# Rotary embedding on one core: the first tile's load in two pieces, both tables behind the first, in place of three pieces with the tables between them

## The chip, the cores and the metric

The kernel runs on one core of one Trainium2 chip. The metric is the device time of one execution in microseconds (us); the time of a kernel is the median of its runs. Before the change it is 169.99 us, the median of 3 runs that went from 169.5 to 170.23.

The engines that matter here are PE (TensorE, matmul), DVE (VectorE), ACT (ScalarE), POOL (GpSimd) and SP (SyncE), which issues every transfer of this kernel. L72 means line 72 of the kernel.

## The reference

```python
def reference(x, cos, sin, num_heads):      # x (16, 512, 1024), cos and sin (512, 32), 16 heads
    x = x.reshape(batch, seq, num_heads, head_dim)          # head_dim 64
    x1, x2 = (x[..., :half_dim].copy(), x[..., half_dim:].copy())
    cos = cos[None, :, None, :].copy()
    sin = sin[None, :, None, :].copy()
    rotated = np.concatenate([x1 * cos - x2 * sin, x1 * sin + x2 * cos], axis=-1)
    return rotated.astype(np.float32)
```

Each output element is its own input times a cosine, plus the element of the other half of its head times a signed sine. Everything is float32: 33.55 MB go in and as much comes out.

## The kernel before

**Tiles and rows.** The input is cut into 8 tiles of 4 MiB, each 128 partitions by 8192 elements. A partition of a tile holds 8 consecutive sequence positions, called rows here (k = 0 to 7), of 1024 elements (4 KB) each. Every instruction of the main loop works on one row over all partitions. Five tile buffers (BUFS) are kept on the chip, so tiles 0 to 4 are loaded ahead of the loop and tiles 5, 6 and 7 when tile 2 has been stored. The result is written over the input in the same buffer and stored from there, a whole tile at once.

**The order of issues on SP.** All loads and stores go through one queue, issued by SP in the order in which the program has them. The first tile is loaded in pieces given by FIRST, (2, 4, 8): rows 0 and 1, then rows 2 and 3, then rows 4 to 7. The two tables, 64 KiB each, stand in between: the order at the start is rows 0-1, sin (L81), rows 2-3, cos (L83), rows 4-7, tile 1, 2, 3, 4. Schedules are written out by hand (manual_schedule): an engine runs its instructions in program order, and waits are put in where data, a buffer or the semaphore of an earlier transfer require it. An instruction waits for the transfer that brings its row, not for the whole tile.

**The tables.** They arrive on 64 partitions and are needed on 128. A matmul with the 64x128 matrix `spread` copies sin (L105) and then cos (L106) into one PSUM tile, `tab`. DVE then makes the signed sine table `sns` in on-chip memory (L108 the negated half, L109 the other half) and copies the two rows of it that DVE itself needs back into `tab` (L113). POOL's first multiply needs `sns`, DVE's first multiply needs `tab`.

**The main loop.** For each row, DVE multiplies by the cosine into PSUM (L158 or L173). The sine product is made by POOL (L155, into a buffer b of the pool `bp`, which has 6 buffers) or, for row 0 and, in odd tiles, row 3 as well, by DVE (L160, in place). The two are added in one of two ways. For the rows in PE_ROWS (0, 3 and 6) PE adds the sine product into PSUM by a matmul with the identity (L163) and ACT copies the sum to the tile (L166). For the other five rows DVE adds (L145), one instruction or more later (the list `pending`). A tile's store (L76) waits for the last of its eight rows.

**At the start PE runs four matmuls on zeros** (L96), which set the PSUM buffers' accumulation flags.

Of the kernel before, what the change touches and what calls it, by code (L numbers as in the profile page):

```python
# [18 lines left out]

DVE_B = ((0,), (0, 3))  # L20

FIRST = (2, 4, 8)
LAST_OUT = (8,)


# [1 line left out]
def kernel(  # L27
# [40 lines left out]
    def load(t, lo=0, hi=KK):  # L68
        if tiles[t] is None:
            tiles[t] = xp.tile([P, F], FP32, name="xt")  # L70
        s = slice(lo * dim, hi * dim)
        nc.sync.dma_start(out=tiles[t][:, s], in_=x_v[t][:, s])  # L72
# [4 lines left out]

    load(0, 0, FIRST[0])
    sin_sb = bp.tile([P, dim], FP32, name="b")[:PB, : KK * half]
    cos_sb = bp.tile([P, dim], FP32, name="b")[:PB, : KK * half]  # L80
    nc.sync.dma_start(out=sin_sb, in_=sin_v)  # L81
    load(0, FIRST[0], FIRST[1])
    nc.sync.dma_start(out=cos_sb, in_=cos_v)  # L83
    for lo, hi in zip(FIRST[1:], FIRST[2:]):
        load(0, lo, hi)
    for t in range(1, BUFS):
        load(t)
# [59 lines left out]
    for t in range(NT):  # L147
# [31 lines left out]
        else:  # L179
            lo = 0  # L180
            for hi in LAST_OUT:
                store(t, lo, hi)
                lo = hi
# [38 lines left out]
```

## Time and profile before

| what | us |
|---|---|
| median of 3 runs | 169.99 |
| the profiled execution's own time | 169.99 |
| its span (first to last instruction) | 167.8 |
| outside the span | 2.2 |
| DVE busy | 139.6 (83% of the span) |
| POOL busy | 121.4 (72%) |
| PE busy | 84.4 (50%) |
| ACT busy | 25.6 (15%) |
| cos table landed | 9.6 |
| first DVE instruction on a table | 10.9 |
| last DVE instruction ends | 154.5 |
| last store issued | 155.6 |

The span is counted from its first instruction. The landing of a transfer is the time at which SP began to issue it, plus the time from issue to landing that the profile lists for it. DVE is the busiest engine and hardly rests between 10.9 and 154.5 us; the transfers are busy for almost as long, and then the last store of 4 MiB stands alone at the end.

### The profile page before, as it was taken

What the parts mean: (1) busy time and instruction counts of PE and PEld (TensorE: products, weight loads), DVE (VectorE), ACT (ScalarE), POOL (GpSimd) and SP (SyncE); (2) the same over time, 40 slices, a digit from 0 to 9 for tenths busy, and PEclk for the clock granted to TensorE, in tenths of its full rate; (3) what the DMA queues carried; (4) which work ended last, traced back from release to release, by engine and by line L of the source; (5) the groups of instructions that cost most, each with busy time, mean ns of one, the idle gap of its engine ahead of it and who ended that gap; (6) DMA issues with size and microseconds to landing.
All of it is one profiled execution on the core that took longest, in us unless ns stands there. A gap on an engine that the chain in (4) does not pass through costs nothing.

```text
span 167.8 us, 612 instructions
## 1 busy us (share of the span) xinstructions
PE 84.4 (50%) x104; PEld 26.4 (16%) x104; DVE 139.6 (83%) x123; ACT 25.6 (15%) x25; POOL 121.4 (72%) x58
## 2 busy tenths in 40 slices
PE   4224618448418834845746184474488408438000
PEld 1111202202102210210221022012022102202000
DVE  1039999999999899999999999999999999997000
ACT  0003220221121122022112202220211220221000
POOL 1019999999999999989796999867996998000000
PEclk9999995585855595555678955765555985585855
DMA  5999999999999999999999999999999999930885
GB/s 187 392 432 473 406 430 437 406 469 398 477 398 438 414 447 422 437 438 406 469 406 461 414 461 406 455 406 437 430 445 422 414 461 398 477 164 0 375 375 250
DMA packets 2754, 67.26 MB, mean 401 GB/s; under 512 B 320, under 2 KB 448, under 8 KB 448
## 3 DMA queue, kind: packets, MB, share of 16 engines
q1 hardware_dynamic: 2752, 67.24, 93.8%
q14 instruction: 2, 0.02, 0.0%
HBM read 33.69 MB, written 33.55 MB: 401 GB/s over the span
## 4 chain that ended last, share of the span: by engine, by line
DVE 70%; issue 13%; DMA 4%; PE 3%; SPq 1%; ACT 1%; DVEq 0%; ACTq 0%
DVE pd L173 28%; DVE xt L145 23%; DVE ps L158 10%; DVE xt L160 9%; DMA b<-in_cos_dram 4%; PE ps L163 2%; PE tab L106 1%; ACT xt L166 1%; SPq L72 1%; SPq L81 0%; DVEq L145 0%; DVE tab L113 0%; DVE sns L108 0%; DVE sns L109 0%; DVEq L160 0%
## 5 line engine op out<-in xcount | busy, mean ns | idle before, releaser
L155 POOL TENSOR_TENSOR b<-xt,sns 128x1024 f32<-128x1024 f32 x52 | 120.7, 2356 | 19.9 <-DVE sns L109 10.5
L163 PE MATMUL ps<-xt,ident 128*128 128x512 f32 x48 | 42.8, 1045 | 34.1 <-issue 20.1
L163 PE MATMUL ps<-b,ident 128*128 128x512 f32 x48 | 37.3, 922 | 29.3 <-DVE ps L158 18.7
L145 DVE TENSOR_TENSOR xt<-pd,b 128x1024 f32<-128x1024 f32 x40 | 48.9, 1221 | 2.9 <-DVE pd L173 0.5
L173 DVE TENSOR_TENSOR pd<-xt,tab 128x1024 f32<-128x1024 f32 x40 | 49.1, 1228 | 1.1
L166 ACT COPY xt<-ps 128x1024 f32<-128x1024 f32 x24 | 24.3, 1012 | 115.2 <-PE ps L163 105.2
L158 DVE TENSOR_TENSOR ps<-xt,tab 128x1024 f32<-128x1024 f32 x24 | 29.3, 1222 | 0.0
L163 PEld LDWEIGHTS ps<-xt,ident 128*128 128x128 f32 x48 | 13.4, 307 | 62.1 <-issue 57.4
L163 PEld LDWEIGHTS ps<-b,ident 128*128 128x128 f32 x48 | 11.6, 266 | 55.6 <-POOL b L155 30.9
L160 DVE TENSOR_TENSOR xt<-xt,tab 128x1024 f32<-128x1024 f32 x12 | 14.6, 1220 | 0.4
L108 DVE TENSOR_SCALAR sns<-tab 128x256 f32<-128x256 f32 x1 | 0.4, 423 | 9.3 <-PE tab L106 9.3
L166 ACT ACT_TABLE_LOAD x1 | 1.3, 1283 | 14.8 <-DVE xt L160 14.8
L105 PE MATMUL tab<-b,spread 64*128 64x256 f32 x2 | 1.2, 696 | 3.0 <-DMA b<-in_sin_dram 3.0
L96 PE MATMUL ps<-zero 128*128 128x512 bf16 x4 | 1.9, 627 | 1.2 <-DVE zero L92 1.2
L106 PE MATMUL tab<-b,spread 64*128 64x256 f32 x2 | 1.2, 710 | 2.4 <-DMA b<-in_cos_dram 2.4
L105 PEld LDWEIGHTS tab<-b,spread 64*128 64x128 f32 x2 | 0.5, 307 | 3.9 <-issue 3.9
L106 PEld LDWEIGHTS tab<-b,spread 64*128 64x128 f32 x2 | 0.5, 306 | 3.2 <-DMA b<-in_cos_dram 3.2
L92 DVE MEMSET zero<- 128x256 uint32 x1 | 0.3, 272 | 0.9 <-PEq L203 0.9
L96 PEld LDWEIGHTS <-zero 128*128 128x128 bf16 x4 | 0.4, 130 | 1.7 <-DVE zero L92 1.2
L113 DVE COPY tab<-sns 128x64 f32<-128x64 f32 x2 | 0.5, 228 | 0.1
L104 DVE COPY spread<-ident 64x64 f32<-64x64 f32 x2 | 0.3, 182 | 0.2 <-POOL ident masks.py:199 0.2
masks.py:197 POOL MEMSET ident<- 128x128 f32 x1 | 0.2, 205 | 0.3 <-POOLq L203 0.3
(6 smaller groups left out, 1.1 us busy)
## 6 DMA issues: line engine op xcount, KB each, us to landing
out_dram<-xt SPq DMA_DIRECT2D x8, 4096.0 KB, 22.6
xt<-in_x_dram SPq DMA_DIRECT2D x7, 4096.0 KB, 29.5
xt<-in_x_dram SPq DMA_DIRECT2D x2, 1024.0 KB, 6.2
xt<-in_x_dram SPq DMA_DIRECT2D x1, 2048.0 KB, 11.4
b<-in_sin_dram SPq DMA_DIRECT2D x1, 64.0 KB, 4.7
b<-in_cos_dram SPq DMA_DIRECT2D x1, 64.0 KB, 7.3
```

The lines of the kernel that those rows point to most:

```text
L72: nc.sync.dma_start(out=tiles[t][:, s], in_=x_v[t][:, s])
L96: nc.tensor.matmul(out=ps[:, c : c + BANK], lhsT=zero[:, :P], rhs=zero, start=True, stop=True)
L105: nc.tensor.matmul(out=sin_t, lhsT=spread, rhs=sin_sb, start=True, stop=True)
L106: nc.tensor.matmul(out=cos_t, lhsT=spread, rhs=cos_sb, start=True, stop=True)
L113: nc.vector.tensor_copy(out=sns_t[:, i * hd : (i + 1) * hd], in_=sns[:, k])
L145: nc.vector.tensor_tensor(out=r, in0=ps, in1=b, op=ALU.add)
L155: nc.gpsimd.tensor_tensor(out=halves(b), in0=swapped(r, nh), in1=over_heads(sk), op=ALU.mult)
L158: nc.vector.tensor_tensor(out=pairs(ps), in0=pairs(r), in1=cos_b(k), op=ALU.mult)
L160: nc.vector.tensor_tensor(out=halves(r), in0=halves(r), in1=swapped_signed(k), op=ALU.mult)
L163: nc.tensor.matmul(out=ps[:, c : c + BANK], lhsT=ident, rhs=rhs, start=False, stop=True, skip_group_check=True)
L166: nc.scalar.copy(out=r, in_=ps)
L173: nc.vector.tensor_tensor(out=pairs(ps), in0=pairs(r), in1=cos_b(k), op=ALU.mult)
```

## The change

FIRST becomes (3, 8): the first tile comes in two pieces, rows 0 to 2 (1.5 MiB) and rows 3 to 7 (2.5 MiB). Both tables are issued behind the first piece, sin and then cos. SP's order at the start is therefore rows 0-2, sin, cos, rows 3-7, tile 1, 2, 3, 4: one transfer fewer, the same bytes in all. The matmul rows, the buffers, the single last store (LAST_OUT, (8,)) and the order of the instructions on PE, DVE, ACT and POOL are the same in both kernels. In the changed kernel, all lines behind L82 have a number lower by one.

```diff
-FIRST = (2, 4, 8)
+FIRST = (3, 8)
 LAST_OUT = (8,)
...
     nc.sync.dma_start(out=sin_sb, in_=sin_v)
-    load(0, FIRST[0], FIRST[1])
     nc.sync.dma_start(out=cos_sb, in_=cos_v)
-    for lo, hi in zip(FIRST[1:], FIRST[2:]):
+    for lo, hi in zip(FIRST, FIRST[1:]):
         load(0, lo, hi)
```

## The prediction

> **What bounds the kernel now.** I read the page first: busy time of each engine over the span, and the transfers' rate.
>
> ```profile
> DVE  1039999999999899999999999999999999997000
> DMA  5999999999999999999999999999999999930885
> GB/s 187 392 432 473 406 430 437 406 469 398 477 398 438 414 447 422 437 438 406 469 406 461 414 461 406 455 406 437 430 445 422 414 461 398 477 164 0 375 375 250
> ```
>
> A slice is 4.2 us. DVE is idle for two slices, then full for 34, then idle while the last store drains. The transfers are full too, but in slices 35 and 36 they run dry and wait for DVE, so they carry a backlog and do not set the end. By windows of 1 us they moved 164 GB/s from 148 to 149 us and nothing from 149 to 154: the backlog ends near 148.4 us, and the last store is issued at 155.6. An earlier end of DVE becomes an earlier end of the kernel, up to some 7 us.
>
> Next, the chain of work that ended last, at its start:
>
> ```profile
> 2.36 7.27 DMA b<-in_cos_dram
> 9.68 1.23 PE tab L106 x2
> 12.24 1.24 DVE ps L158
> 13.51 1.22 DVE xt L160
> ```
>
> The chain starts with the cos table's transfer (landing at 2.36 + 7.27 = 9.63), goes through its matmul, and then lies on DVE until 150.9, where a matmul, a copy and the last store end it. What starts DVE is thus cos. The timeline of the first 32 us shows why sin, which was there earlier, did not help:
>
> ```profile
> 0.73 0.38 SPq L72 DMA_DIRECT2D xt<-in_x_dram  x1
> ...
> 1.17 0.53 SPq L81 DMA_DIRECT2D b<-in_sin_dram  x1
> ...
> 1.74 0.57 SPq L72 DMA_DIRECT2D xt<-in_x_dram  x1
> ...
> 2.36 0.47 SPq L83 DMA_DIRECT2D b<-in_cos_dram  x1
> 2.87 3.10 SPq L72 DMA_DIRECT2D xt<-in_x_dram  x5
> ...
> 6.05 1.19 PE L105 MATMUL tab<-b,spread 64*128 64x256 f32 x2 [2.97 <-DMA b<-in_sin_dram]
> ...
> 9.68 1.22 PE L106 MATMUL tab<-b,spread 64*128 64x256 f32 x2 [2.44 <-DMA b<-in_cos_dram]
> 10.93 0.42 DVE L108 TENSOR_SCALAR sns<-tab 128x256 f32<-128x256 f32 x1 [9.30 <-PE tab L106]
> ...
> 11.77 20.84 POOL L155 TENSOR_TENSOR b<-xt,sns 128x1024 f32<-128x1024 f32 x9 [10.46 <-DVE sns L109]
> ```
>
> L108 reads only the sine, whose matmul ended at 7.24, but it starts at 10.93, after L106: both halves are one tile, and DVE waits for the second matmul. POOL waits behind it. So the end of L106 gates both engines, and it is the quantity to predict.
>
> **Step 1: where the tables land.** The DMA view, one window for each issue, gives the time to landing:
>
> ```profile
> b<-in_sin_dram SPq DMA_DIRECT2D x1, 64.0 KB, 4.7
> b<-in_cos_dram SPq DMA_DIRECT2D x1, 64.0 KB, 7.3
> xt<-in_x_dram SPq DMA_DIRECT2D x1, 2048.0 KB, 11.4
> ```
>
> Sin landed at 5.9 with 1.05 MB ahead of it (1.11 MB with itself), cos at 9.63 behind 2.23 MB in all. Now sin stands behind 1.57 MB, which is 0.52 MB more. Two rates price these. Windows give 394 GB/s for 4 to 8 us: 0.52/0.394 = 1.3 us, sin at 7.2. Between the two landings, 1.11 MB took 3.7 us (300 GB/s): 1.75 us, sin at 7.65. I take 7.4. Cos follows 0.066 MB later, at 0.2 us by either rate: 7.6. Its issue moves up by one place (1.74 in place of 2.36), in time by far.
>
> By the Trainium skill, "DMA: Bandwidth & Descriptors", section "Anatomy of one DMA", a transfer on another issue path costs about 2.0 us and then goes at 436 GB/s; for all 2.23 MB from the first issue that is 0.73 + 2.0 + 5.1 = 7.8 us for cos, where the trace has 9.63. By that estimate cos would now land at 6.6.
>
> **Step 2: the two table matmuls now run back to back.** Before, L105 hid in the wait for cos. Now both are on the path. L105 starts 0.15 us behind its landing (6.05 against 5.9): 7.55. Its two passes have a mean of 696 ns each and end 1.19 after the start, so passes start about 0.5 us apart. Four passes in a row end 3 x 0.5 + 0.7 = 2.2 us after the first start, at 9.75; if L106 must wait for the end of L105, at 7.55 + 1.19 + 1.22 = 9.96. Against cos's own bound, 7.6 + 1.27 = 8.9, the pair decides. I take 9.8, against 10.90 before (9.68 + 1.22). **The gain at the gate is 1.1 us, from 0.7 (sin at 7.65, no overlap) to 1.4 (sin at 7.2, overlap).** It is half or two thirds of the 1.8 to 2.0 us by which cos comes earlier; the rest goes to L105.
>
> A longer pause of PE speaks against this. PE's zeros end at 3.1, so PE rests 2.97 us before L105; now it rests about 4.5. Does that slow the table matmuls? In the same timeline four passes of 512 columns take 1.96 us in one place and 3.75 in another (L163 at 19.74 and 25.85), 0.49 and 0.94 a pass with the last one's drain shared out; half as many columns would be 0.25 and 0.47. The tables' passes start 0.5 us apart, which is already the slow rate, so there is nothing to lose, although the granted-clock column reads 1.00 there. The Trainium skill, "TensorE: Matmul & The Clock Gate", section "Part 1: The HAM clock gate", says that an idle window of about 3.4 us halves the clock; had the pair run at the fast rate before, its estimate would have been another 1.0 us of PE time, and the gain would be nearly nil.
>
> **Step 3: what hides the rest.** Rows 3 to 7 now come as one transfer. Row 3 came with rows 2-3 (1.74 + 7.5 = 9.2); now it lands with row 7, when the same 4.33 MB are through: 2.87 + 11.4 = 14.3. POOL is the first to need it: its third multiply, at 11.77 + 2 x 2.32 = 16.4 before, 15.3 after. DVE needs it at 18.37 - 1.1 = 17.3. The cover is 1.0 us. Behind it POOL has little: row 7's product is ready at 11.77 + 7 x 2.32 = 28.0 and DVE's add of it starts at 28.20, so 0.2 us later everything moves. Cost nothing, while the piece lands before 15.5; this also caps the gain at 16.6 - 14.3 = 2.3 us. Rows 0-2 land before sin in the same queue.
>
> Tiles 1 to 4 keep their bytes ahead of them; tile 1 lands at 3.52 + 20.5 = 24.0 and POOL needs it at 27.9 - 1.1. SP's wait at the fifth of the last group (0.3 us, for an earlier transfer's semaphore) goes, since there is one transfer fewer; that tile is needed near 71, so nothing follows. Tile 5 is closer: issued at 66.36, it lands 25.6 later at 92.0, and POOL starts it at 92.11. The backlog sets that landing, so POOL will not start tile 5 earlier. But its first product is ready at 94.5, and DVE's add of it starts at 104.3: nine microseconds of cover, cost nothing. DVE's and POOL's instructions are the same, 123 and 58, in the same order.
>
> **Step 4: the end.** The last store waits for ACT's copy of row 6 (154.55 to 155.56), behind four matmul passes of 3.57 us at the slow rate (granted 0.50 to 0.55), and for DVE's last add (153.25 + 1.23 = 154.5). Moved by 1.1 us, these matmuls may meet another clock: at the fast rate (1.96 us) ACT would be 1.6 earlier and DVE's add would decide, 1.1 us earlier; at the slow rate of other places (3.75) 0.2 later. I take no change.
>
> **Sum.** 169.99 - 1.1 = 168.9 us. The profiled execution's own time is 169.99, span 167.8 and 2.2 outside it; that is also the median of the three runs, so nothing is corrected.
>
> **Rivals.**
>
> *Small gain.* One of the 16 DMA engines falls behind in the larger first piece, and sin is as late as 7.9 to 8.3. For it: cos landed 0.9 us later than 394 GB/s would make it from sin's landing (5.9 + 1.11/0.394 = 8.7). Each tenth of sin's lateness beyond 7.4 is a tenth of the gain lost, because L105 and L106 hang on it: 168.9 + 0.5 to 168.9 + 0.9, 169.4 to 169.8.
>
> *Larger gain.* As above, and the last matmuls get the fast clock: 168.9 - 1.1 = 167.8. For it: the row of granted clocks flips between 1.0 and 0.5 all along. Against: it is as likely to flip in the runs of before, which lie within 0.7 us.
>
> *Slower: the 2.5 MiB piece lands late.* If it lands at L, POOL's third multiply starts at L, and beyond 15.5 each microsecond is one on DVE's row 7. The time is 168.9 + (L - 15.5): even at 16.6, slower by 0.85 at 17.5. Against: the windows hold 429 and 446 GB/s from 8 to 16 us; landing at 17.5 would need 4.33 MB at 274 GB/s from the first byte near 1.7, against 344 for the landing at 14.3.
>
> *No effect.* The earlier start is absorbed at tile 5 or by the backlog: 170.0. Against: nine microseconds of POOL's lead, and 7 us in which the transfers run dry.
>
> **How the numbers follow.** Forecast 0.55 (168.5 to 169.3); larger gain 0.12; small gain 0.20; no effect 0.05; slower 0.08. A change of 0.5%, 0.85 us, is what a measurement here can tell from none, so faster means below 169.14. Nearly all of the forecast (0.52) and the larger gain make 0.64 faster; 0.03 of the forecast, the small gain and no effect make 0.28 same; 0.08 slower. The range reaches from the larger gain, 167.7, to no effect, 170.0; left out are the slower case and the tails below.
>
> **What would show it.** Sin's landing near 7.4, with L105 and L106 side by side and ending near 9.8; L108 directly behind them, and DVE's first multiply near 11.1 in place of 12.24; no wait for a transfer on POOL's third multiply; DVE's last add ending near 153.4 and the last store issued near 154.5. The prediction is wrong if sin lands after 8.5, if POOL's third multiply shows a wait for the second piece, or if the last store does not move with DVE's start.

## The result, and the profile after

The changed kernel takes 167.96 us (median of 6 runs, 167.07 to 168.68) against 169.82 for the kernel before, run beside it (6 runs, 169.1 to 170.23). The ratio is 0.989, with a 95% interval of 0.985 to 0.993: faster by 1.8 us, 1.2 to 2.5. The prediction was 168.9, faster, with 167.7 to 170.0 as its range. The direction held and the time lies in the range, but the gain is larger than the 1.1 us that were forecast: the time is below the forecast's own band (168.5 to 169.3) and close to the rival with the larger gain (167.8), which had a chance of 0.12.

The profiled execution after took 167.84 us, with a span of 165.7, against 169.99 and 167.8 before: 2.15 us less. Here is where they come from, first in the busy times and the rate of the transfers by slices of 4.1 us:

```profile
DVE  1069999999999999999999999999999999998000
...
DMA  5999989999899998989999899999999999980885
GB/s 187 388 465 401 491 380 498 388 435 451 380 498 388 427 453 388 498 388 475 404 411 475 388 491 396 437 435 403 475 403 467 411 427 443 403 380 0 380 380 253
```

DVE is full again from the third slice on, and it starts a part of a slice earlier (6 in place of 3). The transfers still run dry before the last store (slice 36 moves nothing), so nothing of the earlier start is lost to them. The timeline of the start shows the gate (start, duration, engine and line, and in brackets the idle time before and what ended it):

```profile
1.17 0.53 SPq L81 DMA_DIRECT2D b<-in_sin_dram  x1
...
1.74 0.58 SPq L82 DMA_DIRECT2D b<-in_cos_dram  x1
2.37 2.62 SPq L72 DMA_DIRECT2D xt<-in_x_dram  x5
7.68 1.19 PE L104 MATMUL tab<-b,spread 64*128 64x256 f32 x2 [4.61 <-DMA b<-in_sin_dram]
8.67 1.06 PE L105 MATMUL tab<-b,spread 64*128 64x256 f32 x2
9.77 0.42 DVE L107 TENSOR_SCALAR sns<-tab 128x256 f32<-128x256 f32 x1 [8.14 <-PE tab L105]
...
10.60 23.14 POOL L154 TENSOR_TENSOR b<-xt,sns 128x1024 f32<-128x1024 f32 x10 [9.30 <-DVE sns L108]
11.08 1.23 DVE L157 TENSOR_TENSOR ps<-xt,tab 128x1024 f32<-128x1024 f32 x1
```

The two table matmuls stand side by side and end at 8.67 + 1.06 = 9.73, where the cosine's ended at 10.90 before. DVE's first multiply moves from 12.24 to 11.08, by 1.17 us. POOL runs ten multiplies in one piece: the third finds its rows. The transfers behind this, from the rows of issues (KB, us to landing):

```profile
xt<-in_x_dram SPq DMA_DIRECT2D x1, 2560.0 KB, 11.4
...
b<-in_sin_dram SPq DMA_DIRECT2D x1, 64.0 KB, 6.4
```

Sin lands at 1.17 + 6.4 = 7.6, rows 3 to 7 at 2.37 + 11.4 = 13.8, 1.4 us before POOL's third multiply (10.60 + 2 x 2.31 = 15.2).

The gate explains 1.17 of the 2.15 us. Two more pieces lie further on. The first is a pause of DVE in the middle of the kernel, which the timeline of before has:

```profile
56.18 1.23 DVE L173 TENSOR_TENSOR pd<-xt,tab 128x1024 f32<-128x1024 f32 x1
57.92 1.22 DVE L145 TENSOR_TENSOR xt<-pd,b 128x1024 f32<-128x1024 f32 x1 [0.51 <-DVE pd L173]
```

and the timeline of after has not:

```profile
55.01 1.23 DVE L172 TENSOR_TENSOR pd<-xt,tab 128x1024 f32<-128x1024 f32 x1
56.35 1.23 DVE L144 TENSOR_TENSOR xt<-pd,b 128x1024 f32<-128x1024 f32 x1
```

The add follows the multiply after 0.51 us before and after 0.11 us now. Up to here DVE is 1.17 us ahead, and from here on to the last row 1.57 to 1.58 (the last tile's multiply of row 6 starts at 149.53 before and at 147.95 after). The second piece is the end: from that multiply to the last store's issue it takes 6.06 us before (155.59) and 5.58 after (153.53), because the four matmul passes between them take 3.09 us in place of 3.57; first before, then after:

```profile
150.90 3.57 PE L163 MATMUL ps<-b,ident 128*128 128x512 f32 x4 [2.73 <-DVE ps L158]
149.32 3.09 PE L162 MATMUL ps<-b,ident 128*128 128x512 f32 x4 [2.49 <-DVE ps L157]
```

1.17 + 0.41 + 0.48 is 2.06 us of the 2.1 by which the span is shorter.

So there are three causes to tell apart: the landing of the tables, a pause that I had not seen, and the clock at the end. Each ratio below is against the kernel before, run on the same chip beside it. Its median was 169.56 us beside the four experiments on the gate, 169.81 beside the kernel before with one more write of the zeros and the two kernels with matmuls on zeros at the end, and 170.1 beside the others.

### The profile page after: what moved, and what is told of

Read it like the earlier page. It is cut to its first block, busy times and chain, and to the rows that moved or that the text cites. A ratio compares the mean times of both kernels' runs of the same rounds, so it can differ in the third digit from the quotient of the medians.

```text
span 165.7 us, 609 instructions
## 1 busy us (share of the span) xinstructions
PE 86.7 (52%) x104; PEld 27.1 (16%) x104; DVE 139.6 (84%) x123; ACT 25.6 (15%) x25; POOL 121.4 (73%) x58
## 4 chain that ended last, share of the span: by engine, by line
DVE 71%; issue 13%; DMA 4%; PE 3%; ACT 1%; DVEq 0%; SPq 0%; ACTq 0%
DVE pd L172 29%; DVE xt L144 23%; DVE ps L157 10%; DVE xt L159 9%; DMA b<-in_sin_dram 4%; PE ps L162 2%; PE tab L104 1%; ACT xt L165 1%; PE tab L105 1%; DVEq L144 0%; DVE tab L112 0%; DVE sns L107 0%; SPq L72 0%; DVE sns L108 0%; DVEq L159 0%
## 5 line engine op out<-in xcount | busy, mean ns | idle before, releaser
L162 PE MATMUL ps<-b,ident 128*128 128x512 f32 x48 | 40.0, 980 | 26.6 <-DVE ps L157 16.2
L162 PEld LDWEIGHTS ps<-b,ident 128*128 128x128 f32 x48 | 12.2, 282 | 54.5 <-POOL b L154 29.6
## 6 DMA issues: line engine op xcount, KB each, us to landing
xt<-in_x_dram SPq DMA_DIRECT2D x1, 2560.0 KB, 11.4
```

What stands on the lines that cost most here:

```text
L162: nc.tensor.matmul(out=ps[:, c : c + BANK], lhsT=ident, rhs=rhs, start=False, stop=True, skip_group_check=True)
```

## Experiments on the gate

**Order alone.** Three pieces and as many transfers as before, but cos moved up behind sin:

```diff
     nc.sync.dma_start(out=sin_sb, in_=sin_v)
-    load(0, FIRST[0], FIRST[1])
     nc.sync.dma_start(out=cos_sb, in_=cos_v)
+    load(0, FIRST[0], FIRST[1])
     for lo, hi in zip(FIRST[1:], FIRST[2:]):
```

> Order alone: three pieces as before (rows 0-1, 2-3, 4-7), but both tables behind the first piece. Gate theory (the end of the second table matmul starts DVE and POOL, and it follows the bytes ahead of the tables): sin lands at 5.9 us as before, cos 0.2 later, the pair of table matmuls ends near 8.1 (2.04 us after its start, as in the changed kernel), DVE's first multiply near 9.45 in place of 12.24, rows 4-7 still land (14.3) before POOL's fourth multiply (15.9). Time 169.8 - 2.8 = 167.0, 166.4 to 167.5. Rival (the gain of the change comes from one transfer fewer and larger pieces): as many transfers and the same pieces as before, so 169.8.

Measured: 167.62 us against 169.56, ratio 0.988 (0.985 to 0.991), faster by 2.05 us. The timeline:

```profile
6.46 1.19 PE L105 MATMUL tab<-b,spread 64*128 64x256 f32 x2 [3.39 <-DMA b<-in_sin_dram]
...
7.44 1.06 PE L106 MATMUL tab<-b,spread 64*128 64x256 f32 x2
...
9.86 1.23 DVE L158 TENSOR_TENSOR ps<-xt,tab 128x1024 f32<-128x1024 f32 x1
```

The rival, that the gain comes from fewer and larger transfers, falls for the gate: with the pieces of before, the order alone opens it 2.38 us earlier. (One transfer fewer does play a part of another kind, through the pause; see below.) The expected time was missed by 0.6 us. The gate opened at 9.86, 0.4 later than the 9.45 expected, since sin landed at 1.15 + 5.2 = 6.35 and not at 5.9. The pause is there again (0.53 us, at 55 us), as in the kernel before, so it has no part in the miss.

**Pieces alone.** The two pieces of the change, with cos behind both:

```diff
-    nc.sync.dma_start(out=cos_sb, in_=cos_v)
     for lo, hi in zip(FIRST, FIRST[1:]):
         load(0, lo, hi)
+    nc.sync.dma_start(out=cos_sb, in_=cos_v)
```

> Pieces alone: two pieces (rows 0-2, rows 3-7), sin behind the first, cos behind the second. Gate theory: cos lands at about 14.4 us, its matmul ends near 15.7 in place of 10.9, DVE and POOL start 4.8 us later than in the kernel before: 174.6, 174.0 to 175.2. Rival (pieces and transfer count carry the gain): 168 to 169, as in the changed kernel.

Measured: 173.53 us, ratio 1.024 (1.020 to 1.028), slower by 4.0 us.

```profile
13.81 1.22 PE L105 MATMUL tab<-b,spread 64*128 64x256 f32 x2 [5.18 <-DMA b<-in_cos_dram]
...
16.39 1.23 DVE L157 TENSOR_TENSOR ps<-xt,tab 128x1024 f32<-128x1024 f32 x1
```

Cos landed at 2.36 + 11.4 = 13.8, 0.6 earlier than expected, so the time stayed below the expected 174.0 to 175.2. DVE's first multiply came at 16.39, 4.15 us later than before. Within its interval (3.3 to 4.7 us) the time follows the cosine's landing one for one.

**Two PSUM tiles.** The order of before, with the sine in a tile and bank of its own, so that DVE's sine instructions need not wait for the cosine's matmul:

```diff
-    sin_t = tab[:, KK * half : 2 * KK * half]
+    tab2 = pfix.tile([P, BANK], FP32, name="tab2")
+    sin_t = tab2[:, : KK * half]
...
-    sns_t = tab[:, KK * half : KK * half + len(on_dve) * hd]
+    sns_t = tab2[:, : len(on_dve) * hd]
```

> The kernel before, with its order of transfers, but the sine and the cosine table in two PSUM tiles in two banks. Gate theory (DVE's first sine instruction, which reads only the sine, waits for the cosine's matmul because both are one tile): it starts near 7.3 us in place of 10.93, POOL near 8.1 in place of 11.77, and DVE's first multiply directly behind the cosine's matmul, at 10.95 in place of 12.24: 169.8 - 1.3 = 168.5, 168.1 to 169.0. Rival (the wait is for the cosine itself or for the bank's neighbour, and the tile doesn't matter): 169.8.

Measured: 168.44 us, ratio 0.993 (0.990 to 0.995), faster by 1.2 us.

```profile
7.33 0.42 DVE L109 TENSOR_SCALAR sns<-tab 128x256 f32<-128x256 f32 x1 [5.72 <-PE tab L106]
...
8.17 6.95 POOL L156 TENSOR_TENSOR b<-xt,sns 128x1024 f32<-128x1024 f32 x3 [6.88 <-DVE sns L110]
...
11.02 1.23 DVE L159 TENSOR_TENSOR ps<-xt,tab 128x1024 f32<-128x1024 f32 x1 [2.40 <-PE tab L107]
```

DVE's sine instruction starts at 7.33 in place of 10.93, right behind the sine's matmul (L106 here), and POOL 3.6 us earlier. What held it before was that both tables were one tile, in one bank; this run changes tile and bank together and does not tell them apart. DVE's first multiply comes 1.22 us earlier, by the four small instructions that used to stand between.

**How late rows 3 to 7 may come.** The changed kernel with a smaller first piece and so a larger second one:

```diff
-FIRST = (3, 8)
+FIRST = (2, 8)
```

> The changed kernel with FIRST (2, 8): rows 0-1, both tables, then rows 2-7 in one transfer of 3 MiB. Gate theory with the cover of step 3: the gate opens near 8.1 us and DVE's first multiply is near 9.45, but rows 2-7 land at 14.3 and POOL's second multiply, wanted at 11.3, waits 3 us for them; row 7's product is ready at 14.35 + 6 x 2.32 = 28.3, so DVE's add of row 7 comes at 28.3 as before (28.2): 169.9, 169.3 to 170.3. Rival (only the gate counts, POOL has slack enough): 167.0. Rival (fewer transfers carry the gain): 168, as in the changed kernel.

Measured: 169.33 us, ratio 1.000 (0.998 to 1.002): no gain.

```profile
9.38 2.34 POOL L154 TENSOR_TENSOR b<-xt,sns 128x1024 f32<-128x1024 f32 x1 [8.07 <-DVE sns L108]
...
14.14 16.21 POOL L154 TENSOR_TENSOR b<-xt,sns 128x1024 f32<-128x1024 f32 x7 [2.42 <-DMA xt<-in_x_dram]
...
21.14 1.22 DVE L144 TENSOR_TENSOR xt<-pd,b 128x1024 f32<-128x1024 f32 x1 [1.55 <-POOL b L154]
...
28.07 1.23 DVE L144 TENSOR_TENSOR xt<-pd,b 128x1024 f32<-128x1024 f32 x1 [0.92 <-POOL b L154]
```

The gate opens as early as with the order alone (DVE's first multiply at 9.85), but POOL's second multiply waits 2.42 us for row 2, and DVE gives back 1.55 + 0.92 = 2.47 us in two waits for POOL: the whole gain of the gate, 2.39. This is the slower rival of the prediction, made real by moving one row: POOL has next to no lead in the first tile. With three rows in the first piece the change stays on the right side of it by 1.4 us.

## Experiments on the pause, the end and a better start

**The pause.** It is in the profile of before, of the order alone and of the two PSUM tiles, and not in those of after, of the pieces alone and of (2, 8). The first three load the first tile in three pieces, the others in two. DVE's list in the trace holds, besides its 123 instructions, waits for semaphores as entries of their own, ahead of the instruction that waits: 55 of them in the first three kernels (178 entries in all), 53 or 54 in the others (176 or 177). In the first three the pause stands between the 63rd and the 64th entry of this list, which are a wait and its add. Nothing but the place was moved by writing the zeros once more on DVE, in the time in which it waits for the tables:

```diff
     nc.vector.memset(zero, 0.0)
+    nc.vector.memset(zero, 0.0)
```

First the kernel before with this line, and nothing else:

> The kernel before with one more write of the zeros on DVE and nothing else. Theory of the instruction's place: the pause of 0.5 us near 57 us goes, the gate stays at 12.24: 169.9 - 0.5 = 169.4, 169.0 to 169.6. Rival (the pause belongs to data or transfers): 169.9. With it, the part of the change's 1.8 us that comes from the count of DVE's waits is measured alone.

Measured: 169.38 us, ratio 0.998 (0.995 to 1.000), faster by 0.4 us, just clear of none. The pause is gone from the timeline, with the gate at 12.22:

```profile
56.17 1.23 DVE L174 TENSOR_TENSOR pd<-xt,tab 128x1024 f32<-128x1024 f32 x1
57.50 1.23 DVE L146 TENSOR_TENSOR xt<-pd,b 128x1024 f32<-128x1024 f32 x1
```

Then the order alone with the same line:

> The first experiment (three pieces, both tables behind the first) with one instruction more on DVE at the start: the zeros are written twice (0.27 us, while DVE waits for the tables anyway). Theory of the instruction's place: the 0.5 us pause of DVE near 55 us stands in the three kernels with three pieces, always between the 63rd and 64th instruction that DVE lists (a semaphore wait and the add behind it); one instruction more puts another pair there and the pause goes: 167.6 - 0.5 = 167.1, 166.6 to 167.5, DVE without a pause over 0.2 us from 16 us on. Rival (the pause comes from the data, a product of POOL or a transfer that is late): the pause stays near 55 us, 167.6.

Measured: 166.98 us, ratio 0.982 (0.980 to 0.984), against 0.988 without the line; no pause. The medians stand 0.6 us apart (167.62 and 166.98), the ratios 1.0 us, since the kernel before was 0.5 us slower beside this run. And the changed kernel with two such lines, which bring the pair of wait and add back to the 63rd and 64th place:

> The changed kernel with two instructions more on DVE at the start (the zeros are written three times), which puts the same pair of wait and add at the 63rd and 64th place as in the kernel before. Theory of the instruction's place: a pause of 0.5 us near 56 us comes in, 168.0 + 0.45 = 168.4, 168.0 to 168.8. Rival (data, or the count of transfers): no pause, 168.0.

Measured: 168.71 us, ratio 0.992 (0.989 to 0.995), against 0.989 (0.985 to 0.993) without them, 0.5 us slower. These intervals overlap, so the time alone would not settle it; the timeline does, for the pause has come in:

```profile
54.94 1.23 DVE L174 TENSOR_TENSOR pd<-xt,tab 128x1024 f32<-128x1024 f32 x1
56.68 1.23 DVE L146 TENSOR_TENSOR xt<-pd,b 128x1024 f32<-128x1024 f32 x1 [0.52 <-DVE pd L174]
```

It can be switched off and on by the place of an instruction, with the same data, transfers and buffers. In the thirteen profiles of this study it stands in all six that have a wait at the 63rd place and its add at the 64th, and in none of the other seven. What the engine does at that place is not shown by any run.

**The end.** Matmuls on zeros fill PE's pauses in the last tile of the kernel before:

```diff
+    warm = pfix.tile([P, BANK], FP32, name="warm")
...
+                if t == NT - 1 and k < PE_ROWS[-1]:
+                    for _ in range(8):
+                        nc.tensor.matmul(out=warm, lhsT=zero[:, :P], rhs=zero, start=True, stop=True)
                 nc.scalar.copy(out=r, in_=ps)
```

> The kernel before with eight matmuls on zeros after row 0 and eight after row 3 of the last tile, into a PSUM bank of their own, which fill PE's pauses there (2.4 and 2.7 us). Theory of the end (the granted clock of the last four matmul passes sets when ACT's copy of row 6 ends, and with it the last store): PE keeps the high clock, the four passes take about 2 us in place of 3.57, ACT ends before DVE's last add, and the store is issued behind that add: 1.0 us earlier, 169.9 - 1.0 = 168.9, 168.6 to 169.3. Rival (the clock at the end changes nothing that counts, or the added matmuls delay the last four): 169.9 or up to 170.7.

Measured: 169.45 us, ratio 0.997 (0.995 to 1.000), faster by 0.5 us (0.1 to 0.8) where 1.0 was expected.

```profile
146.31 1.89 PE L169 MATMUL warm<-zero 128*128 128x512 bf16 x8
150.64 2.79 PE L164 MATMUL ps<-b,ident 128*128 128x512 f32 x4 [2.44 <-DVE ps L159]
```

The four passes take 2.79 us in place of 3.57, not the 2 that were expected: the granted clock is 1.00 until 151 us and 0.66 on the mean from 151 to 153. PE was idle for 2.4 us between the two groups, and the clock fell in the middle of the second. From DVE's multiply of row 6 to the last store it took 5.28 us in place of 6.06. This makes the expected mechanism likely, with half the effect, but does not show it beyond doubt: in the eleven profiles without these matmuls the four passes take between 3.09 us (the changed kernel, the shortest) and 3.75, and in the last kernel below, which has them, 3.24.

**Tables first.** The reading of the gate, carried on: both tables ahead of all rows, and smaller pieces, so that POOL's second row isn't late:

```diff
-FIRST = (2, 4, 8)
+FIRST = (2, 3, 5, 8)
...
-    load(0, 0, FIRST[0])
     sin_sb = bp.tile([P, dim], FP32, name="b")[:PB, : KK * half]
     cos_sb = bp.tile([P, dim], FP32, name="b")[:PB, : KK * half]
     nc.sync.dma_start(out=sin_sb, in_=sin_v)
-    load(0, FIRST[0], FIRST[1])
     nc.sync.dma_start(out=cos_sb, in_=cos_v)
-    for lo, hi in zip(FIRST[1:], FIRST[2:]):
+    for lo, hi in zip((0,) + FIRST, FIRST):
         load(0, lo, hi)
```

> Both tables are issued ahead of all rows, and the first tile comes in pieces of rows 0-1, 2, 3-4, 5-7. Gate theory: with nothing ahead of them the tables land at 3 to 4 us, their matmuls end by 6, and then the first piece decides: issued at 1.9 in place of 0.73, it lands near 7.0, DVE's first multiply follows at 7.05 in place of 12.24. POOL gets row 2 at 8.3 and never waits long: its product of row 7 is ready 16.2 us after 7.0, 0.3 later than DVE wants it. 169.6 - 5.2 + 0.3 = 164.7, 164.0 to 165.4. Rival (the transfers' backlog, which ran dry at 148.4 us before the last store at 155.6, sets the end, since the rows now start 1.1 us later and there are two transfers more): 166 or more, with no time between the backlog and the last store.

Measured: 164.94 us, ratio 0.970 (0.967 to 0.972), faster by 5.2 us and the best of all.

```profile
3.17 1.19 PE L103 MATMUL tab<-b,spread 64*128 64x256 f32 x2
4.15 1.06 PE L104 MATMUL tab<-b,spread 64*128 64x256 f32 x2
5.25 0.42 DVE L106 TENSOR_SCALAR sns<-tab 128x256 f32<-128x256 f32 x1 [3.62 <-PE tab L104]
...
7.05 1.23 DVE L156 TENSOR_TENSOR ps<-xt,tab 128x1024 f32<-128x1024 f32 x1 [0.53 <-DMA xt<-in_x_dram]
7.10 6.97 POOL L153 TENSOR_TENSOR b<-xt,sns 128x1024 f32<-128x1024 f32 x3 [5.80 <-DMA xt<-in_x_dram]
```

The gate is now the first piece of rows, with 0.53 us of wait; the tables are no longer what DVE waits for.

**Tables on another queue.** To save the 1.2 us by which the rows' first issue was later, ACT issues the tables, at the same time as SP the rows; besides, two PSUM tiles and the second write of the zeros.

```diff
-    nc.sync.dma_start(out=sin_sb, in_=sin_v)
-    nc.sync.dma_start(out=cos_sb, in_=cos_v)
+    nc.scalar.dma_start(out=sin_sb, in_=sin_v)
+    nc.scalar.dma_start(out=cos_sb, in_=cos_v)
```

> The parts that worked, together: tables issued by ACT at the same time as SP issues rows 0-1, 2, 3-4, 5-7; sine and cosine in two PSUM tiles; the zeros written twice. Gate theory: tables land at 3.5 to 4.5 us, rows 0-1 near 5.9, DVE's first multiply at 6.3 to 6.8 in place of 12.24, no pause of 0.5: 169.6 - 5.7 - 0.4 = 163.5, 162.8 to 164.3. Rival (backlog of the transfers sets the end): 165 or more.

Measured: 166.29 us, ratio 0.978 (0.976 to 0.980). The expectation failed. The time is one that the rival allowed, but its reason does not hold: the transfers still rest before the last store (no packet began from 149 to 152 us). The rows of issues:

```profile
xt<-in_x_dram SPq DMA_DIRECT2D x1, 1024.0 KB, 5.0
b<-in_sin_dram ACTq DMA_DIRECT2D x1, 64.0 KB, 5.3
b<-in_cos_dram ACTq DMA_DIRECT2D x1, 64.0 KB, 6.3
```

Issued at 0.74 and 1.31, the tables landed at 6.0 and 7.6, where on SP's queue with nothing ahead they took 2.3 and 2.2 us and landed at 3.0 and 3.5. The second queue did not carry them past the rows; DVE's first multiply came at 8.91. The Trainium skill, "DMA: Bandwidth & Descriptors", section "Issuing engines are not separate DMA queues", says that transfers of all issuing engines run on the same 16 engines and interleave. Here the interleaving came late: 64 KB took 5.3 us beside 1 MiB that took 5.0, and by 4.7 us SP's queue had moved 123 packets (1.01 MB) and ACT's none; only from then to 7.2 us did both move. Why ACT's queue began so late is not shown.

**All that worked.** Tables first in SP's queue, with the second write of the zeros and the matmuls on zeros at the end.

> The fastest kernel so far (tables ahead of all rows, pieces of rows 0-1, 2, 3-4, 5-7) with one more write of the zeros on DVE, which moves the pair of wait and add off the 63rd and 64th place, and with the matmuls on zeros in the last tile. If the three effects add up: 164.9 - 0.5 (pause) - 0.6 to 1.0 (end) = 163.6, 163.2 to 164.5. If the end is set by the transfers' backlog by now: 164.4 or more.

Measured: 165.09 us, ratio 0.974 (0.970 to 0.977): the effects no longer add up, and the second case of the expectation holds. The slices of 4.1 us:

```profile
DMA  3999999999899999999999999999999999999983
GB/s 68 415 431 497 417 401 489 393 441 457 385 473 304 475 409 417 473 393 457 441 385 417 473 393 449 441 395 425 457 401 449 441 425 441 425 425 453 401 385 144
```

The transfers no longer run dry before the last store (it is issued at 150.2 and follows the backlog without a gap). In the kernel with the tables first a short rest was left: no packet began from 150 to 151 us, where here 164 GB/s move. There the last store was issued at 150.62 and the span is 162.7; here it is issued 0.42 us earlier and the span is 163.6. So an earlier end of DVE bought nothing any more: the bound has passed to the transfers, and the next step would have to shorten those.

## Why the prediction was right, and where it fell short

**What bounds.** Right. The time follows the gate, measured at DVE's first multiply: 2.4 us earlier gives 2.05 (order alone), 1.2 earlier gives 1.2 (two PSUM tiles), 4.15 later gives 4.0 (pieces alone), 5.2 earlier gives 5.2 (tables first). The stretch in which the transfers are dry was put at 7 us and is nearer 5 (the windows count a packet where it begins): in the trace of before the last packet of the backlog ends at 150.2, and the store is issued at 155.6.

**Step 1, where the tables land.** Right. Sin was put at 7.4 and landed at 7.6, between the 7.2 and 7.65 of the two rates. Cos was put at 7.6 and landed at 1.74 + 6.1 = 7.8; the other estimate, 6.6, was too early.

**Step 2, the pair of matmuls.** Right. Its end was put at 9.8 and came at 9.73; a gain of 1.1 us was taken, 1.17 came. PE rested 4.61 us in place of 2.97 and the sine's matmul still took 1.19 us, as before. The clock rule that the prediction cites cost nothing here. This fits the reason given, that the pair was at the slow rate already: with the tables first PE rests only 0.1 us before the pair, and the sine's matmul takes the same 1.19 us.

**Step 3, the covers.** Right for the transfers. Rows 3 to 7 landed 0.5 us earlier than put, and POOL did not wait. Tile 5's rows did hold POOL up (2.66 us of idle time, its first multiply at 91.98 as at 92.11 before), and this cost DVE nothing. The step's last sentence is the one that failed: "DVE's and POOL's instructions are the same, 123 and 58, in the same order." The count is right, but it leaves out the waits that DVE runs. One piece fewer took two of them out, and everything behind moved by two places; the pause of 0.5 us went with it. It was in the profile of before as one line of 0.5 us among the waits, and the prediction did not ask what it was. Measured alone, it is worth 0.4 us (ratio 0.998, 0.995 to 1.000).

**Step 4, the end.** No change was taken, with up to 1.1 us earlier named as open. 0.48 came in the profiled execution. That this end can move the time is made likely by the matmuls on zeros (0.997, just clear of none). How much of the 1.8 us between the medians is due to it is open: the passes at the end take 3.09 to 3.75 us from kernel to kernel, and nothing in the change sets them.

**The sum.** 1.1 was put for the gate and 1.17 came; to it the pause adds 0.4. The remaining 0.2 to 0.3 us of the median's gain are within its interval of 1.2 to 2.5 us. So the term for the gate was right to 0.1 us, the pause was a term that the sum put at nothing, because the count of instructions was the same, and the time left the forecast's band on that side. The rival of a larger gain named the end alone and reached 167.8; that the time came near it was in part luck, for it came by two causes of which the rival named one. The rival with late rows was right in its mechanism and its price, as the kernel with (2, 8) shows, and it did not decide because the cover was 1.4 us.

## What to carry to other kernels

Look for the transfer that opens the gate for the busiest engine, count the bytes that stand ahead of it in its queue, and put small tables ahead of large pieces; then check which engine has the least lead behind the gate, because it says how large the next piece may be. A single wait that no data explains, even half a microsecond, may hang on the place of an instruction; moving it by one place is a cheap test. When the gains stop adding up, look at whether the transfers still run dry somewhere.

## What was not expected of the hardware

- A pause of DVE of 0.51 to 0.54 us that comes and goes with the place of a wait and its add (63rd and 64th entry that DVE lists); worth 0.4 to 0.5 us of the time.
- Sin lands later where cos follows it in the queue than where rows do. With rows 0-1 ahead it took 4.7 to 4.8 us from issue to landing where rows follow (four profiles) and 5.2 where cos follows (three); with rows 0-2 ahead 6.1 (one) against 6.3 and 6.4. No run was made for the cause.
- A table of 64 KB on a second queue, issued at the same time as 1 MiB on the first, landed later than that 1 MiB (5.3 us against 5.0); its queue moved nothing before 4.7 us.
